# Product 6's weights multiplied by the gate on GpSimd, the last scaling on two engines, and one group of sums moved to GpSimd

## The chip, the cores and the metric

The kernel runs on one core of a Trainium2 chip. The metric is device time in microseconds; 957.09 is the median of three runs of the kernel before (956.73 to 957.37). The engines are TensorE (PE in the profile, its weight loads PEld), VectorE (DVE), ScalarE (ACT), GpSimd (POOL) and SyncE (SP), which here only issues DMA transfers.

## What is computed

One layer of a diffusion backbone on 512 tokens of 1024 channels with 256 context tokens. The attention and convolution ahead of the last part are left out here; the change touches only the MLP at the end, where `ga2` is one gate for each channel:

```
x = x + ga1 * (y_lat @ w_o)
x = x + ga2 * (square(relu(modulate(x, g_norm2, sh2, sc2) @ w_up)) @ w_down)
return rmsnorm(x, g_final)
```

## The kernel before

All products of this part are float32, each as three matmuls of rounded parts: an operand is split into a high part (rounded to fp32r by ScalarE) and a low part (what is left, by VectorE), and `mm3` issues high x high, high x low, low x high. So each weight tile, 128x1024, is loaded by SyncE into one of four raw buffers (`NRAW`), rounded by ScalarE, subtracted by VectorE, and read by TensorE from one of five pairs of buffers (`NW`): `weights`, lines 126 to 135.

The two MLP products are done as 2x2 block schemes with seven products in the place of eight, so that sums of blocks are multiplied. In the **up stage** (some 636 to 798 us) `left_sums` (line 1095) makes four sums of the normalized tokens' blocks for each of two pairs of token tiles, m = 0 and m = 1, by four VectorE subtractions or additions of 128x512, each depending on the one before for the first three; `keep` then splits them. The weights' own sums are made by `up_sum` (line 504): two on GpSimd (lines 510, 514), two on VectorE, in place.

The **down stage** (798 us to the end) has products n = 0 to 6, each of eight blocks of weights p = 0 to 7, here called p0 to p7, with 12 matmuls of 512 columns a block (`product`, line 1303). Sums of weights for n = 2, 3, 5 and 6 were made in device memory beforehand by `weight_sums`; `down_weights` (line 489) loads the right one. The stream of weights runs three blocks ahead in program order, and four raw buffers and five split buffers set how far ahead a load, a rounding and a subtraction can start. Left parts (`ap`) are split from the activations in `left_parts` in the same way, on the same two engines.

Product 6 adds only to tokens of the upper half (token tiles 2 and 3) and channels 0 to 511. Its last four blocks (`LAST`) are kept, and TensorE runs them first for token tile 2 (`ps_dd`), then for channels 0 to 255 of token tile 3, then, in a bank of their own (`ps_e`), for channels 256 to 511. Behind each, VectorE multiplies the sum in PSUM by the gate (`ada[5][0]`), adds it to the residual `x1`, ScalarE squares and sums for the norm, VectorE multiplies by `g_final`. `rstd_col` gives the reciprocal root as two factors, `y3` and `t3`, and two VectorE instructions scale the token tile's halves by both; SyncE issues the store of half 0 and ScalarE that of half 1 (lines 1379 to 1405).

Where nothing else is said, the order of the instructions on an engine is set when the program is built, from readiness and priorities, so it need not be the order of the lines. `tc.high_priority` moves instructions forward; `pinned` keeps some in the order of the lines.

Of the kernel before, what the change touches and what calls it, by code (L numbers as in the profile page):

```python
# [8 lines left out]
F32 = mybir.dt.float32  # L9
# [3 lines left out]
AF = mybir.ActivationFunctionType  # L13
ALU = mybir.AluOpType

P = 128
# [34 lines left out]
def hybrid_block_kernel(  # L51
# [6 lines left out]
    nc = tc.nc  # L58
    x, ctx, w_ada, w_in = x[0], ctx[0], w_ada[0], w_in[0]
    conv_w, w_conv_out, w_gla_out, w_o = conv_w[0], w_conv_out[0], w_gla_out[0], w_o[0]  # L60
    w_up, w_down, b_in, b_ada, out = w_up[0], w_down[0], b_in[0], b_ada[0], out[0]

    const = es.enter_context(tc.tile_pool(name="const", bufs=1))
    sp = es.enter_context(tc.tile_pool(name="sp", bufs=4))
# [25 lines left out]
    act, dve, pe = Engine(nc.scalar), Engine(nc.vector), Engine(nc.tensor)  # L90
# [4 lines left out]
    def kblk(name, dt=F32):  # L95
        return kp.tile([P, 512], dt, tag="kb", name=name)
# [6 lines left out]
    def psum(name):  # L103
        return pp.tile([P, 512], F32, tag="ps", name=name)

    def raw_tile(name):
        return wp.tile([P, 1024], F32, tag="raw", name=name, bufs=NRAW)
# [4 lines left out]
    def split(src, hi, lo, keep=False):  # L112

        for ins in (act.copy(out=hi, in_=src),
                    dve.tensor_tensor(out=lo, in0=src, in1=hi.bitcast(F32), op=ALU.subtract)):
            if keep:
                pinned(ins)
# [5 lines left out]

    latest = [None]

    def weights(name, src):

        raw = raw_tile("r_" + name)
        a, b = src.shape[1], src.shape[2]
        nc.sync.dma_start(out=raw.rearrange("p (a b) -> p a b", a=a), in_=src)  # L130
        hi = wp.tile([P, 1024], F32R, tag="hi", name="h_" + name)
        lo = wp.tile([P, 1024], F32R, tag="lo", name="l_" + name)
        split(raw, hi, lo, name == "up")
        latest[0] = lo
        return hi.rearrange("p (a b) -> p a b", a=a), lo.rearrange("p (a b) -> p a b", a=a)
# [29 lines left out]
    def rstd_col(name, first, last, n):  # L165

        b, v, y, t = (sp.tile([P, 1], F32, tag="rc_" + i, name=f"{i}_{name}") for i in "bvyt")
        dve.tensor_scalar(out=b, in0=first, scalar1=1.0 / n, scalar2=EPS, op0=ALU.mult, op1=ALU.add)
        act.activation(out=t, in_=last, func=AF.Ln, scale=1.0 / n, bias=b)
        act.activation(out=y, in_=t, func=AF.Exp, scale=-0.5)  # L170
        dve.scalar_tensor_tensor(out=v, in0=last, scalar=1.0 / n, in1=b, op0=ALU.mult, op1=ALU.add)
        dve.scalar_tensor_tensor(out=t, in0=y, scalar=y, in1=v, op0=ALU.mult, op1=ALU.mult)
        dve.tensor_scalar(out=t, in0=t, scalar1=-0.5, scalar2=1.5, op0=ALU.mult, op1=ALU.add)
        return y, t
# [75 lines left out]
    def sum_sq(dst, src, eng):  # L250
        junk = kp.tile([P, src.shape[1]], BF16, tag="junk", name="junk", bufs=2)
        if eng is act:
            act.activation(out=junk, in_=src, func=AF.Square, accum_out=dst)
        else:
            dve.scalar_tensor_tensor(out=junk, in0=src, scalar=1.0, in1=src, op0=ALU.mult, op1=ALU.mult, accum_out=dst)
# [131 lines left out]
    for s in range(2):  # L387
        dve.tensor_copy(out=lr_sel[:, 64 * s:64 * s + 48].rearrange("p (i r) -> p i r", i=3),
                        in_=sel[:, 16 * s:16 * s + 16].unsqueeze(1).to_broadcast([P, 3, RANK]))
    ps = psum("ps_c")  # L390
# [18 lines left out]
    ps = psum("ps_va")  # L409
# [17 lines left out]
    mod_w[1] = [ada_raw(1, q) for q in range(2)]  # L427
    normalized(x_tok, r_x, 0, P)
    wq = weights("q0", cols(w_in, C_Q))
    key_weights(1)  # L430
    Engine.ordered = False
# [37 lines left out]
    t_sum = [[dp.tile([P, 2, 512], F32, tag=f"t{i}_{p}", name=f"t{i}_{p}") for p in range(NFF // 4)] for i in range(4)]  # L469
# [3 lines left out]
    def quarter(j, hf, p):  # L473
        return rows(w_down, 16 * j + 2 * p, 512 * hf)

    def weight_sums():
# [7 lines left out]
        for i, p, src, add in todo:  # L484
            pinned(nc.gpsimd.tensor_copy(out=tick, in_=latest[0][0:1, 0:1].bitcast(F32)))
            pinned(nc.gpsimd.dma_start(out=t_sum[i][p], in_=src, **({"accum_op": ALU.add} if add else {})))  # L486
            yield

    def down_weights(n, p):

        if n in (2, 3, 5, 6):
            return weights("dn", t_sum[{2: 0, 3: 2, 5: 1, 6: 3}[n]][p])
        return weights("dn", quarter(*{0: (1, 0), 1: (0, 0), 4: (1, 1)}[n], p))

    up_raws = {}
# [69 lines left out]
    plan += [("up", cols(w_up, f * P)) for f in EARLY]  # L565
    hold = len(plan)
    plan += [("dn", lambda n=n, p=p: down_weights(n, p)) for n in range(7) for p in range(NFF // 4)]
    ws = Stream(plan, 3, hold)

# [240 lines left out]
    ada = {}  # L810
# [61 lines left out]
    def project(name, act=None):  # L872
        wt = ws.take(name)
        ps = tiles(name, act or h_lat, wt)
        ws.free()
        return ps
# [135 lines left out]
    for j in range(KT):  # L1012
        ps = project("go", og)
# [7 lines left out]
    x1 = [[None, None] for _ in range(MT)]  # L1021
# [73 lines left out]
    def left_sums(m):  # L1095

        (a11, a12), (a21, a22) = h2_f[m], h2_f[m + 2]
        s1, s2, s3, s4 = (kblk(f"s{i}").rearrange("p (k c) -> p k c", k=KH) for i in range(4))
        for out, a, b, op in ((s1, a21, a22, ALU.subtract), (s2, s1, a11, ALU.subtract),
                              (s4, s2, a12, ALU.add), (s3, a11, a21, ALU.subtract)):  # L1100
            dve.tensor_tensor(out=out, in0=a, in1=b, op=op)
        return s1, s2, s3, s4

    for m in range(MT):
# [14 lines left out]
    up_weights(0, "ua")  # L1119
    second_h(MT - 1, prev)  # L1120
    s_f = [left_sums(m) for m in range(2)]
    bp.release()
    mp = es.enter_context(tc.tile_pool(name="mp", bufs=1, reuse_waits="tile"))
# [173 lines left out]
    def block(ps, m, lp, wt, i, cs, start, stop, more=False):  # L1297
        mm3(ps, lp[0][:, i, m, :], lp[1][:, i, m, :], wt[0][:, i, cs], wt[1][:, i, cs], start, stop, more=more)
# [19 lines left out]
    def pair(name):  # L1318
        return [psum(name) for _ in range(2)]
# [55 lines left out]
    ps_d = pair("ps_dd")  # L1375
# [3 lines left out]
    for mi in range(2):  # L1379
        m, last = 2 + mi, mi == 1  # L1380
        pieces = [(0, 256), (256, 512)] if last else [(0, 512)]
        tmp = mp.tile([P, 2, 512], F32, tag="sp", name="tail", bufs=4)[:, 0, :] if last else kblk("tail")
        for i, (c0, c1) in enumerate(pieces):
            cs = slice(c0, c1)
            ps, x2, tt = ps_d[mi][:, cs], x1[m][0][:, cs], tmp[:, cs]
            if i == 1:

                dve.tensor_tensor(out=tt, in0=ps, in1=ada[5][0][:, cs], op=ALU.mult)
                dve.tensor_tensor(out=x2, in0=x2, in1=tt, op=ALU.add)
                ps = psum("ps_e")[:, cs]  # L1390
            for b in range(LAST):
                for j in range(2):
                    block(ps, mi, parts[b], wd[b], j, cs, i == 1 and b + j == 0, b == LAST - 1 and j == 1)
            with tc.high_priority(offset=100):
                dve.tensor_tensor(out=tt, in0=ps, in1=ada[5][0][:, cs], op=ALU.mult)
                dve.tensor_tensor(out=x2, in0=x2, in1=tt, op=ALU.add)
                sum_sq(ss3[:, m, i + 1:i + 2], x2, act)
                if i == 1:
                    dve.tensor_tensor(out=ss3[:, m, 0:1], in0=ss3[:, m, 0:1], in1=ss3[:, m, 1:2], op=ALU.add)
                dve.tensor_tensor(out=x2, in0=x2, in1=gf[0][:, cs], op=ALU.mult)  # L1400
        with tc.high_priority(offset=100):
            y3, t3 = rstd_col("n3", ss3[:, m, 0:1], ss3[:, m, i + 1:i + 2], D)
        for hf in range(2):
            dve.tensor_scalar(out=x1[m][hf], in0=x1[m][hf], scalar1=y3, scalar2=t3, op0=ALU.mult, op1=ALU.mult)
            (nc.sync, act)[hf].dma_start(out=out[m * P:(m + 1) * P, hf * 512:(hf + 1) * 512], in_=x1[m][hf])


# [27 lines left out]
```

## Time and profile before

| | us |
|---|---|
| median of three runs | 957.09 |
| lowest, highest | 956.73, 957.37 |
| the profiled execution | 959.36 |
| its span, first to last instruction | 957.6 |
| TensorE busy in it | 940.1 |
| VectorE busy | 710.2 |
| ScalarE busy | 536.2 |
| GpSimd busy | 164.8 |

The profile shows one execution; its own time is 1.8 us longer than its span and 2.3 us over the median. Times in the rows are microseconds from the span's start, engines have the names PE, PEld, DVE, ACT, POOL and SP. `r_dn`, `h_dn` and `l_dn` are a down weight tile as loaded, its high and its low part; `x1b` is the residual, `acc` the gate, `gf` the final norm's weights, `x_tmp` and `tail` products with the gate. A matmul's end is modelled, and pipelined matmuls overlap in the rows. What ended an engine's idle time stands in brackets behind a row.

### The profile page before, as it was taken

How to read it: one execution, taken by the hardware profiler on the slowest of the kernel's cores; microseconds unless marked ns; L12 is line 12 of the kernel's file. 1: busy time of each engine (PE TensorE's matmuls, PEld its weight loads, DVE VectorE, ACT ScalarE, POOL GpSimd, SP SyncE). 2: the span in 40 equal slices, each digit the busy share in tenths (PEclk: the TensorE clock that was granted, in tenths of full speed). 3: DMA queues.
4: the chain of work that ended last, by engine and by line, in shares of the span. 5: the costliest groups of instructions: out<-in, count | busy, mean ns of one | idle time of the engine just before them, and what ended most of it. 6: DMA issues, size and time to landing. Idle time of an engine off the chain costs nothing.

```text
span 957.6 us, 14834 instructions
## 1 busy us (share of the span) xinstructions
PE 940.1 (98%) x5555; PEld 800.1 (84%) x5555; DVE 710.2 (74%) x1170; ACT 536.2 (56%) x1008; POOL 164.8 (17%) x231
## 2 busy tenths in 40 slices
PE   6999999999999999999999999999999999999996
PEld 4678888788888888888888888899999998888886
DVE  5366685888598859977566484688768778899896
ACT  5476453745565556743543332478777687656662
POOL 8011022132112200002000000122445540000000
PEclk9999999999999999999999999999999999999999
DMA  9784072989648843636538466322557859655661
GB/s 288 225 293 169 5 250 74 233 188 192 172 132 215 172 120 103 206 98 181 184 95 261 130 216 202 130 88 63 189 169 177 188 128 309 227 191 190 196 220 44
DMA packets 162040, 165.51 MB, mean 173 GB/s; under 512 B 7524, under 2 KB 126416, under 8 KB 161712
## 3 DMA queue, kind: packets, MB, share of 16 engines
q1 hardware_dynamic: 147248, 124.94, 43.3%
q0 software_dynamic: 13568, 37.53, 15.9%
q10 hardware_dynamic: 1152, 2.10, 0.6%
q8 instruction: 43, 0.70, 0.3%
q14 instruction: 29, 0.24, 0.1%
HBM read 160.35 MB, written 37.75 MB: 207 GB/s over the span
## 4 chain that ended last, share of the span: by engine, by line
PE 91%; DVE 3%; DMA 3%; ACT 1%; issue 1%; SPq 0%; POOL 0%; DVEq 0%; POOLq 0%; ACTq 0%
PE ps_ua L83 8%; PE ps_da L83 7%; PE ps_v L83 6%; PE ps_c L83 5%; PE ps_ga L83 5%; PE ps_b L83 5%; PE ps_xa L83 5%; PE ps_r L83 5%; PE ps_y L83 5%; PE ps_db L83 5%; PE ps_gb L83 5%; PE ps_go L83 5%; PE ps_uc L83 4%; PE ps_co L83 4%; PE ps_dc L83 2%; PE ps_k L83 2%
## 5 line engine op out<-in xcount | busy, mean ns | idle before, releaser
L83 ACT CAST h_dn<-r_dn 128x1024 fp32r<-128x1024 f32 x56 | 59.0, 1054 | 48.0 <-PE ps_da L83 20.5
L83 DVE TENSOR_TENSOR l_dn<-r_dn,h_dn 128x1024 fp32r<-128x1024 f32 x56 | 68.1, 1221 | 14.7 <-ACT h_dn L83 14.4
L83 PE MATMUL ps_da<-h_dn,ap 128*128 128x512 f32 x192 | 59.6, 389 | 0.0
L83 DVE SCALAR_TENSOR_TENSOR acc<-wa,silu_c,acc 128x512 f32<-128x512 f32 x64 | 45.8, 747 | 12.4 <-DMA wa<-in_w_ada_dram 10.1
L83 PEld LDWEIGHTS ps_da<-h_dn,ap 128*128 128x128 f32 x192 | 36.0, 188 | 7.5
L486 POOL DMA_DIRECT2D t<-in_w_down_dram x48 | 40.3, 864 | 4.0 <-issue 3.9
L83 PE MATMUL ps_db<-h_dn,ap 128*128 128x512 f32 x128 | 39.8, 389 | 0.0
L83 PE MATMUL ps_da<-l_dn,ap 128*128 128x512 f32 x96 | 37.3, 389 | 0.0
L83 DVE TENSOR_TENSOR ap<-ug,ap 128x512 fp32r<-128x512 f32 x56 | 36.2, 685 | 0.0
L514 POOL TENSOR_TENSOR r_up<-r_up,r_up 128x512 f32<-128x512 f32 x14 | 24.3, 1737 | 48.3 <-DVE r_up L83 42.8
L83 ACT CAST ap<-ug 128x512 fp32r<-128x512 f32 x56 | 31.9, 617 | 0.3 <-DVE t_n L83 0.3
L1067 POOL DMA_DIRECT2D x<-x x8 | 4.4, 545 | 155.1 <-DVE x L83 152.3
L83 PEld LDWEIGHTS ps_db<-h_dn,ap 128*128 128x128 f32 x128 | 24.0, 188 | 4.9
L510 POOL TENSOR_TENSOR r_up<-r_up,r_up 128x512 f32<-128x512 f32 x14 | 25.9, 1852 | 6.2 <-DMA r_up<-in_w_up_dram 6.2
L83 PE MATMUL ps_v<-h_v,hh 128*128 128x512 f32 x64 | 25.8, 403 | 0.0
L83 PE MATMUL ps_xa<-hh,h_xa 128*128 128x512 f32 x64 | 25.5, 398 | 0.0
L83 PE MATMUL ps_ga<-hh,h_ga 128*128 128x512 f32 x64 | 25.4, 397 | 0.0
L83 PE MATMUL ps_b<-hh,h_b 128*128 128x512 f32 x64 | 25.4, 396 | 0.0
L83 PE MATMUL ps_c<-hh,h_c 128*128 128x512 f32 x64 | 25.3, 396 | 0.0
L83 PE MATMUL ps_co<-yah,h_co 128*128 128x512 f32 x64 | 25.2, 394 | 0.0
L83 PE MATMUL ps_r<-hh,h_r 128*128 128x512 f32 x64 | 25.1, 392 | 0.0
L83 PE MATMUL ps_y<-h_wo,yh 128*128 128x512 f32 x64 | 25.1, 392 | 0.0
(526 smaller groups left out, 3391.3 us busy)
## 6 DMA issues: line engine op xcount, KB each, us to landing
t<-in_w_down_dram POOLq DMA_DIRECT2D x48, 512.0 KB, 7.9
wa<-in_w_ada_dram SPq DMA_DIRECT2D x32, 512.0 KB, 4.1
r_up<-in_w_up_dram SPq DMA_DIRECT2D x32, 512.0 KB, 4.2
r_dn<-t SPq DMA_DIRECT2D x32, 512.0 KB, 4.1
r_dn<-in_w_down_dram SPq DMA_DIRECT2D x24, 512.0 KB, 4.4
wa<-in_w_ada_dram SPq DMA_DIRECT2D x32, 256.0 KB, 4.7
t<-t POOLq DMA_DIRECT2D x16, 512.0 KB, 5.6
r_v<-in_w_in_dram SPq DMA_DIRECT2D x8, 512.0 KB, 5.0
```

The lines of the kernel that those rows point to most:

```text
L83: ins = op(*args, **kwargs)
L486: pinned(nc.gpsimd.dma_start(out=t_sum[i][p], in_=src, **({"accum_op": ALU.add} if add else {})))
L510: pinned(nc.gpsimd.tensor_tensor(out=b0, in0=a0, in1=b0, op=ALU.add))
L514: pinned(nc.gpsimd.tensor_tensor(out=a0, in0=b1, in1=a0, op=ALU.subtract))
L1067: nc.gpsimd.dma_start(out=x1_d[m][:, hf, :], in_=x1[m][hf])
```

## The change

Three edits. (1) Product 6's weights are multiplied by the gate in their raw buffer, by two GpSimd instructions of 128x512 for each of the eight blocks, between the load and the rounding; the sums in PSUM of product 6 are then added to the residual without a product with the gate. (2) For the last token tile the two factors of the reciprocal root are multiplied with each other first, and then VectorE scales half 0 and ScalarE half 1. (3) `left_sums` runs on GpSimd for m = 0 and stays on VectorE for m = 1.

```diff
--- before.py
+++ after.py
@@ -123,11 +123,13 @@
 
     latest = [None]
 
-    def weights(name, src):
+    def weights(name, src, change=None):
 
         raw = raw_tile("r_" + name)
         a, b = src.shape[1], src.shape[2]
         nc.sync.dma_start(out=raw.rearrange("p (a b) -> p a b", a=a), in_=src)
+        if change:
+            change(raw)
         hi = wp.tile([P, 1024], F32R, tag="hi", name="h_" + name)
         lo = wp.tile([P, 1024], F32R, tag="lo", name="l_" + name)
         split(raw, hi, lo, name == "up")
@@ -486,10 +488,14 @@
             pinned(nc.gpsimd.dma_start(out=t_sum[i][p], in_=src, **({"accum_op": ALU.add} if add else {})))
             yield
 
+    def gated(raw):
+        for i in range(2):
+            nc.gpsimd.tensor_tensor(out=raw[:, i * 512:(i + 1) * 512], in0=raw[:, i * 512:(i + 1) * 512], in1=ada[5][0], op=ALU.mult)
+
     def down_weights(n, p):
 
         if n in (2, 3, 5, 6):
-            return weights("dn", t_sum[{2: 0, 3: 2, 5: 1, 6: 3}[n]][p])
+            return weights("dn", t_sum[{2: 0, 3: 2, 5: 1, 6: 3}[n]][p], gated if n == 6 else None)
         return weights("dn", quarter(*{0: (1, 0), 1: (0, 0), 4: (1, 1)}[n], p))
 
     up_raws = {}
@@ -1098,7 +1104,7 @@
         s1, s2, s3, s4 = (kblk(f"s{i}").rearrange("p (k c) -> p k c", k=KH) for i in range(4))
         for out, a, b, op in ((s1, a21, a22, ALU.subtract), (s2, s1, a11, ALU.subtract),
                               (s4, s2, a12, ALU.add), (s3, a11, a21, ALU.subtract)):
-            dve.tensor_tensor(out=out, in0=a, in1=b, op=op)
+            (nc.gpsimd if m == 0 else dve).tensor_tensor(out=out, in0=a, in1=b, op=op)
         return s1, s2, s3, s4
 
     for m in range(MT):
@@ -1379,29 +1385,33 @@
     for mi in range(2):
         m, last = 2 + mi, mi == 1
         pieces = [(0, 256), (256, 512)] if last else [(0, 512)]
-        tmp = mp.tile([P, 2, 512], F32, tag="sp", name="tail", bufs=4)[:, 0, :] if last else kblk("tail")
         for i, (c0, c1) in enumerate(pieces):
             cs = slice(c0, c1)
-            ps, x2, tt = ps_d[mi][:, cs], x1[m][0][:, cs], tmp[:, cs]
+            ps, x2 = ps_d[mi][:, cs], x1[m][0][:, cs]
             if i == 1:
 
-                dve.tensor_tensor(out=tt, in0=ps, in1=ada[5][0][:, cs], op=ALU.mult)
-                dve.tensor_tensor(out=x2, in0=x2, in1=tt, op=ALU.add)
+                dve.tensor_tensor(out=x2, in0=x2, in1=ps, op=ALU.add)
                 ps = psum("ps_e")[:, cs]
             for b in range(LAST):
                 for j in range(2):
                     block(ps, mi, parts[b], wd[b], j, cs, i == 1 and b + j == 0, b == LAST - 1 and j == 1)
             with tc.high_priority(offset=100):
-                dve.tensor_tensor(out=tt, in0=ps, in1=ada[5][0][:, cs], op=ALU.mult)
-                dve.tensor_tensor(out=x2, in0=x2, in1=tt, op=ALU.add)
+                dve.tensor_tensor(out=x2, in0=x2, in1=ps, op=ALU.add)
                 sum_sq(ss3[:, m, i + 1:i + 2], x2, act)
                 if i == 1:
                     dve.tensor_tensor(out=ss3[:, m, 0:1], in0=ss3[:, m, 0:1], in1=ss3[:, m, 1:2], op=ALU.add)
                 dve.tensor_tensor(out=x2, in0=x2, in1=gf[0][:, cs], op=ALU.mult)
         with tc.high_priority(offset=100):
             y3, t3 = rstd_col("n3", ss3[:, m, 0:1], ss3[:, m, i + 1:i + 2], D)
+        if last:
+            dve.tensor_tensor(out=t3, in0=t3, in1=y3, op=ALU.mult)
         for hf in range(2):
-            dve.tensor_scalar(out=x1[m][hf], in0=x1[m][hf], scalar1=y3, scalar2=t3, op0=ALU.mult, op1=ALU.mult)
+            if last and hf:
+                act.activation(out=x1[m][hf], in_=x1[m][hf], func=AF.Copy, scale=t3)
+            elif last:
+                dve.tensor_scalar(out=x1[m][hf], in0=x1[m][hf], scalar1=t3, scalar2=None, op0=ALU.mult)
+            else:
+                dve.tensor_scalar(out=x1[m][hf], in0=x1[m][hf], scalar1=y3, scalar2=t3, op0=ALU.mult, op1=ALU.mult)
             (nc.sync, act)[hf].dma_start(out=out[m * P:(m + 1) * P, hf * 512:(hf + 1) * 512], in_=x1[m][hf])
 
 

```

## Rows read from the trace of the kernel before

**Rows 1.** The page, first part: busy us, share of the span and instructions of each engine.

```profile
PE 940.1 (98%) x5555; PEld 800.1 (84%) x5555; DVE 710.2 (74%) x1170; ACT 536.2 (56%) x1008; POOL 164.8 (17%) x231
```

**Rows 2.** Chain that ended last, in order of time: start us, us, engine, tile, matmuls.

```profile
906.55 21.76 PE ps_da L83 x96
```

**Rows 3.** Timeline of PE in the up stage: start us, us, instruction [idle before <-releaser].

```profile
661.17 0.39 PE L83 MATMUL ps_uc<-s4h,h_ub 128*128 128x256 f32 x1 [0.72 <-ACT uq L83]
```

**Rows 4.** Timeline of SP, product 6's first load; last line of the view of tile r_dn.

```profile
909.75 0.32 SPq L130 DMA_DIRECT2D r_dn<-t  x1
...
DMA to landing us min/median/max: 3.1/4.3/7.5
```

**Rows 5.** Timeline of ACT: rounding of block p7's weights.

```profile
936.55 1.05 ACT L83 CAST h_dn<-r_dn 128x1024 fp32r<-128x1024 f32 x1 [1.46 <-issue]
```

**Rows 6.** Timeline of DVE: low parts of the weights p4 and p5, and of p7.

```profile
935.17 2.35 DVE L83 TENSOR_TENSOR l_dn<-r_dn,h_dn 128x1024 fp32r<-128x1024 f32 x2
...
939.78 1.22 DVE L83 TENSOR_TENSOR l_dn<-r_dn,h_dn 128x1024 fp32r<-128x1024 f32 x1
```

**Rows 7.** Timeline of PE: start of block p7, and the last matmul of the kernel.

```profile
942.88 0.62 PE L83 MATMUL ps_dd<-h_dn,ap 128*128 128x512 f32 x2
...
950.10 0.28 PE L83 MATMUL ps_e<-h_dn,ap 128*128 128x256 f32 x1
```

**Rows 8.** Busy us by stretch: PE, PEld, DVE, ACT, POOL, PEclk; last: tile ps_da alone.

```profile
636.00:661.00 25.00, 24.44 (x205) 24.24 (x203) 23.14 (x34) 19.39 (x42) 8.96 (x3) 1.00 0.25 71
912.85:941.00 28.15, 28.15 (x126) 23.32 (x125) 26.51 (x38) 15.27 (x22) 0.00 (x0) 1.00 0.51 169
28.00:32.00 4.00, 2.72 (x29) 1.42 (x27) 1.73 (x5) 1.94 (x4) 0.00 (x0) 1.00 1.11 337
32.00:36.00 4.00, 4.00 (x13) 3.17 (x12) 2.06 (x4) 3.16 (x6) 0.00 (x0) 0.57 1.02 316
...
912.85:941.00 28.15, 15.46 (x69) 12.47 (x67) 2.64 (x4) 1.00 0.51 169
```

**Rows 9.** Timeline of POOL: four of its 28 additions and subtractions in the up stage.

```profile
637.75 4.97 POOL L510 TENSOR_TENSOR r_up<-r_up,r_up 128x512 f32<-128x512 f32 x1 [5.54 <-DMA r_up<-in_w_up_dram]
...
656.25 2.28 POOL L510 TENSOR_TENSOR r_up<-r_up,r_up 128x512 f32<-128x512 f32 x1
...
670.95 1.31 POOL L510 TENSOR_TENSOR r_up<-r_up,r_up 128x512 f32<-128x512 f32 x1
...
769.10 2.27 POOL L510 TENSOR_TENSOR r_up<-r_up,r_up 128x512 f32<-128x512 f32 x1
```

**Rows 10.** Timeline of DVE around three of them.

```profile
640.88 0.68 DVE L83 TENSOR_TENSOR s<-s,h2f 128x512 f32<-128x512 f32 x1
...
642.08 1.19 DVE L83 TENSOR_TENSOR h2l<-h2f,h2h 128x512 fp32r<-128x512 f32 x1 [0.51 <-ACT h2h L83]
...
657.41 2.21 DVE L83 TENSOR_TENSOR l_uc<-r_up,h_uc 128x1024 fp32r<-128x1024 f32 x1
...
770.15 0.41 DVE L83 TENSOR_TENSOR uq<-uq,ps_ub 128x256 f32<-128x256 f32 x1
```

**Rows 11.** Groups of DVE, 912.94 to 941.00: line, operation, tiles xcount | busy us, mean ns.

```profile
L83 DVE TENSOR_TENSOR x1b<-x1b,x_tmp 128x512 f32<-128x512 f32 x4 | 2.6, 680 | 0.0
...
L83 DVE TENSOR_TENSOR x_tmp<-q,acc 128x512 f32<-128x512 f32 x2 | 1.4, 682 | 0.0
...
L83 DVE TENSOR_TENSOR x1b<-x1b,gf 128x512 f32<-128x512 f32 x2 | 1.3, 684 | 0.0
```

**Rows 12.** Timeline of DVE behind the last matmul; one ACT instruction of 128x512.

```profile
950.71 0.42 DVE L83 TENSOR_TENSOR tail<-ps_e,acc 128x256 f32<-128x256 f32 x1
...
952.73 0.22 DVE L83 SCALAR_TENSOR_TENSOR t_n<-y_n,v_n 128x1 f32<-128x1 f32 x1
...
953.17 1.00 DVE L83 TENSOR_SCALAR x1b<-x1b,y_n,t_n 128x512 f32<-128x512 f32 x2
...
946.18 0.63 ACT L83 ACTIVATE junk<-x1b 128x512 bf16<-128x512 f32 x1 [8.58 <-DVE x1b L83]
```


## The prediction, written before the change was run

> **What bounds the kernel now.** I read the page's first part, then the chain that ended last, then single stretches. TensorE is busy for 98% of the span [rows 1], and in the down stage the chain holds nothing but its matmuls, as in the 21.76 us of product 5 from 906.55 on [rows 2]. So a change there costs time when it makes TensorE wait, and saves time only behind the last matmul. The up stage has one TensorE wait left, 0.72 us at 661.17 [rows 3].
>
> The edit that matters is the multiplication of product 6's weights. Their way is: load, round to the high part on ScalarE, subtract to the low part on VectorE, matmul. Block p0's load is issued at 909.75 and such loads land after 3.1 us at the earliest [rows 4], so at 912.85. The last block's (p7) rounding starts at 936.55 and takes 1.05 [rows 5], its low part starts at 939.78 and ends at 941.00 [rows 6], and TensorE begins p7 at 942.88 [rows 7]. p7's low part is first read by the second matmul, 0.23 later: a slack of 2.1 us. Between 912.85 and 941.00, 28.15 us, TensorE never stops and VectorE is busy for 26.51 [rows 8].
>
> **What a GpSimd instruction costs VectorE.** GpSimd does the same form today, a 128x512 add of two tiles of the on-chip memory. Undisturbed it takes 1.31 us [rows 9]. At 656.25 one takes 2.28 [rows 9], and VectorE's low-part subtraction at 657.41, which has two such inputs as well, takes 2.21 [rows 10] instead of the 1.22 of this shape [rows 6]: VectorE loses 0.99 us to it. At 637.75 a GpSimd add that starts in a run of VectorE subtractions takes 4.97 us [rows 9]; the run's last starts at 640.88, the add comes through in VectorE's idle 0.51 us behind it, and the next subtraction, at 642.08, takes 1.19 where its form takes 0.68 [rows 10]. At 770.15 a VectorE instruction with one input from PSUM keeps its 0.41 us while a GpSimd add, from 769.10 to 771.37, lies over it [rows 9, 10]. So the two engines take turns where both read two tiles of the on-chip memory, at about 1.0 us of VectorE's time for a GpSimd instruction, and GpSimd has to wait while VectorE runs without a gap.
>
> **The change, part by part.**
>
> *Weights times gate.* 8 blocks by 2 halves are 16 GpSimd instructions, 16 x 0.99 = 15.8 us of shared reading. VectorE's own is 26.51 less the 2.64 that read PSUM [rows 8], 23.9. Together 39.7 us have to pass in a stretch of 28.15, an overrun of 11.55. Less the slack of 2.1 this is 9.45. Behind the last GpSimd product p7 must still be rounded (1.05 [rows 5]), when neither side has other work for the shared reading: 10.5. Below that: 0, if the 16 x 1.31 = 21.0 us ran freely in the 23.7 us between 912.85 and p7's rounding. Above: 16 x 1.31 taken from VectorE in full, 21.0 + 23.9 - 28.15 - 2.1 + 1.05 = 15.7. I take 10.5, since row and count are of this very form. Queued behind a GpSimd product on GpSimd is only the next one; on ScalarE everything behind the block's rounding waits (the next left parts and squared sums), and VectorE's low part behind that; the low part frees the buffer of the load four blocks on, so p4 to p7 land later as well. No load is added, and SP's queue keeps its order. TensorE is hurt from p4 on: five pairs of buffers let the first blocks be split up to four blocks, 10.9 us, ahead.
>
> The row at 637.75 and a page of the Trainium skill part here. SBUF — State Buffer, section "SBUF: two separate sides", says that the pair of ports is a lock and that whoever starts first gets it for a whole instruction; the subtraction of 640.88 started 3.1 us later than the add of 637.75 and yet went first. By the page's order GpSimd would never wait for more than one VectorE instruction, its products would finish sooner, and the roundings behind the last would lie beside VectorE work: the term would be 9.45 and not 10.5.
>
> *Clock.* If TensorE stands still its clock may fall. At 28 to 32 us TensorE was busy for 2.72 of 4 us, and the granted clock of the next 4 us reads 0.57 [rows 8], nearly all at the lower level, 1.2 GHz: (1 - 0.57) x 4 = 1.7 us lost. Here p3 would end near 939, 3 x 1.36 before p7's start of 942.88 (1.36 being half of a block's 2.72, since in the tail token tile 2 goes first), and p4 begin some 8 us later. Part of the loss would hide, as p5 to p7 wait for their low parts anyway. Between 0 and 1.7 I take 0.8.
>
> *Left sums.* Four VectorE subtractions of 0.68 (the form of [rows 11]) leave, 2.7 us; four GpSimd ones come, 4 x 0.99 = 4.0: the shared reading grows by 1.3 us in a stretch where VectorE is busy for 23.14 of 25.00 us [rows 8]. Behind them in GpSimd's queue stands the add of 637.75, behind the sums the splits, and VectorE's and ScalarE's chain to the wait at 661.17. If the shorter VectorE queue wins, the 0.72 us goes; if all GpSimd time lands on the chain, +4.0. I take +0.8: the net growth of 1.3, less a part for the stretch's 1.86 us of idle VectorE, some of which it can use.
>
> *Tail.* The last matmul ends at 950.38 [rows 7]. VectorE begins the product with the gate at 950.71, as its earlier two products of this kind keep it busy, and the add that follows 0.46 later [rows 12]. Both earlier products and this one go, so the add can begin at 950.41: -0.76. One more 128x1 instruction comes, at 0.25 (the pitch from the one at 952.73 to the next), and the two scalings, 1.00 in sequence on VectorE from 953.17 [rows 12], become one on VectorE beside one on ScalarE of 0.63 (the same shape at 946.18 [rows 12]): -0.37. Together -0.9. The two stores behind them are issued on the same queues as now. What the third product that goes (token tile 2's) saves counts for nothing: TensorE's matmuls of token tile 3 cover it.
>
> **Sum.** 10.5 + 0.8 + 0.8 - 0.9 = +11.2 us. The profiled execution took 959.36 us for a span of 957.6, so it would be 970.6; it stands 2.3 us over the median of the runs, 957.09, and from that I come to **968.3 us**. Own range of this case: low 957.09 + 8 - 0.7 + 0 - 0.9 = 963.5 (a GpSimd instruction at 0.83 us: 13.3 + 23.9 - 28.15 - 2.1 + 1.05 = 8.0); high, with half of the way to the upper ends, 957.09 + 13.1 + 1.3 + 2.4 - 0.9 = 973.0.
>
> **Rivals.**
>
> *It fits (not slower).* The 21.0 us of GpSimd work lie in 23.7 us, and both engines run side by side: then only the tail is left, 956.2, and 955.5 if the wait at 661.17 goes as well. It decides if a GpSimd product costs VectorE less than 0.33 us: then 16 x 0.33 + 23.9 is no more than 28.15 + 2.1 - 1.05. For it: undisturbed, each block needs 2.62 us, and TensorE takes 2.72 for one (21.76 / 8 [rows 2]). Against: the 2.21 and the 4.97, and VectorE's only 1.64 us of idle.
>
> *VectorE's order softens it.* The finishing of product 5 (four adds, two products and two scalings with both inputs on chip, 2.6 + 1.4 + 1.3 = 5.3 us [rows 11]) now stands ahead of p4's low part at 935.17 [rows 6]. If it came behind the splits in the changed program, 5.3 of the overrun would fall where TensorE doesn't wait: 10.5 - 5.3 + 0.8 - 0.9 = +5.1, 962.2. For it: nothing but product 6's end needs these. Against: their inputs are ready at 927.9, sooner than any late weight, so an order by readiness puts them first.
>
> *Left sums alone decide.* If the weights fit but the left sums do not, +4.0 - 0.9 = +3.1, 960.2; one step of the above, at a small chance.
>
> **How the numbers follow.** Forecast 0.63, order 0.13, left sums alone 0.04, it fits 0.20. No change that a measurement tells is within 0.2%, 1.9 us. It fits gives 956.2, within that; faster needs more than the tail and the 0.72 together (1.6), so 0.04 of its 0.20, and same 0.16. Slower 0.80. The range 956 to 974 takes in the rivals down to 956.2 and the forecast's own range; it leaves out the fastest 0.04 and some 0.12 of the forecast beyond 974, where two upper ends would meet.
>
> **What would show it.** Right: TensorE idle by some 9 us in the last product, before p4 to p7, waiting for l_dn; VectorE's l_dn of p0 to p7 well over 1.22 us each; GpSimd products with a median near 2 us; VectorE full from 912 to 952. Wrong: GpSimd products of 1.31 beside l_dn of 1.22. In the tail the last add right behind the last matmul, and both stores issued within 0.1 us. For the left sums the wait that stood at 661.17, longer or gone.

## The result, and the profile after

The changed kernel takes **973.36 us** (median; 973.0 to 976.85) beside 956.91 for the kernel before: ratio 1.0178, 95% interval 1.0157 to 1.0199. On a second chip it took 971.57 beside 957.83, ratio 1.0137 (1.0113 to 1.0161). Forecast were 968.3 and slower: the sign is right, the mechanism in the main, and the loss of 11.2 was sized too small; measured are 16.5 and 13.7. The first of the two times lies 0.4 above the forecast's own range (963.5 to 973.0), the second within it. The two profiled executions of the changed kernel, with spans of 971.2 and 968.6, are called the first and the second trace.

How the traces are compared matters here. Taking the start of each matmul in one trace less its start in the trace of before, the first 40 us alone differ between executions by 0.7 to 2.9 us, in kernels that do the same there (the profiled execution of before has the slow stretch of [rows 8] at 32 us, the others don't). From 40 us on the offset changes only at a few places, and it is counted from there below (us):

| | left sums (at 668) | down products 0 to 5 | last product, to its last matmul | behind it |
|---|---|---|---|---|
| changed, first trace | +1.8 | +0.7 | +13.6 | -0.55 |
| changed, second trace | +1.9 | 0.0 | +12.5 | -0.55 |

The first trace's sum is 15.5, the second's 13.8. The last product holds most of both. The 0.7 is a step at 796.46, where TensorE waits 0.35 us for an `ap` of ScalarE; it isn't the left sums', since a kernel further down that has them on VectorE shows such a wait too (0.34 at 794.33), and why it comes only in some executions is open. The page of after, part 1 and the new group of part 5 (busy us, mean ns | idle before, releaser); they answer to [rows 1]:

```profile
PE 942.1 (97%) x5555; PEld 800.1 (82%) x5555; DVE 720.4 (74%) x1162; ACT 537.2 (55%) x1009; POOL 201.0 (21%) x251
...
L493 POOL TENSOR_TENSOR r_dn<-r_dn,acc 128x512 f32<-128x512 f32 x16 | 31.8, 2021 | 127.2 <-DMA r_dn<-t 124.7
```

VectorE has 8 instructions fewer and is busy for 10.2 us more. In the last product TensorE waits for it; first the timeline of PE of before, where p4's low part is first read, then that of after, waits only (start, us [idle before <- releaser]):

```profile
939.26 0.39 PE L83 MATMUL ps_dd<-l_dn,ap 128*128 128x512 f32 x1
```

```profile
938.26 0.50 PE L83 MATMUL ps_dd<-l_dn,ap 128*128 128x512 f32 x1 [0.96 <-DVE l_dn L83]
...
950.85 0.79 PE L83 MATMUL ps_dd<-l_dn,ap 128*128 128x512 f32 x1 [9.57 <-DVE l_dn L83]
```

The first wait is for the low part of block p3, the second for that of p4. In the second trace the two waits are 0.31 and 9.56. What VectorE did until then, timeline of DVE of after:

```profile
923.05 1.28 DVE L83 TENSOR_TENSOR ap<-ug,ap 128x512 fp32r<-128x512 f32 x2
927.85 1.23 DVE L83 TENSOR_TENSOR l_dn<-r_dn,h_dn 128x1024 fp32r<-128x1024 f32 x1 [3.51 <-ACT h_dn L83]
931.35 1.23 DVE L83 TENSOR_TENSOR l_dn<-r_dn,h_dn 128x1024 fp32r<-128x1024 f32 x1 [2.27 <-ACT h_dn L83]
932.49 3.48 DVE L83 TENSOR_TENSOR ap<-ug,ap 128x512 fp32r<-128x512 f32 x2
935.89 2.31 DVE L83 TENSOR_TENSOR l_dn<-r_dn,h_dn 128x1024 fp32r<-128x1024 f32 x1
...
940.53 2.85 DVE L83 TENSOR_TENSOR x1b<-x1b,x_tmp 128x512 f32<-128x512 f32 x2
943.30 1.75 DVE L83 TENSOR_TENSOR x_tmp<-q,acc 128x512 f32<-128x512 f32 x1
944.97 0.68 DVE L83 TENSOR_TENSOR x_tmp<-ps_da,acc 128x512 f32<-128x512 f32 x1
...
949.58 2.34 DVE L83 TENSOR_TENSOR l_dn<-r_dn,h_dn 128x1024 fp32r<-128x1024 f32 x2
```

The pair `ap` at 932.49 takes 3.48 where the pair at 923.05, undisturbed, takes 1.28, the single `l_dn` at 935.89 2.31 and not 1.22, `x_tmp` from `q` 1.75 and not 0.68: each instruction loses 1.07 to 1.10 us. The `x_tmp` at 944.97, which reads PSUM, keeps its 0.68, and the pair of `l_dn` at 949.58, behind the last GpSimd product, its 2.34 [rows 6]. GpSimd's products in the view of tile r_dn of after (ns min/median/max):

```profile
L493 POOL TENSOR_TENSOR r_dn<-r_dn,acc x16: 1290/1728/5796, 913.5 to 946.1; 128x512 f32<-128x512 f32 x16
```

The one of 5.8 us began at 919.69, while VectorE ran without a gap from 918.86 to 924.3. The roundings behind it came late, and for them VectorE stands idle 3.51 and 2.27 us in the rows above. The clock, after, by stretch (columns as in [rows 8], the granted clock is the third from the right):

```profile
944.00:948.00 4.00, 0.00 (x0) 0.00 (x0) 4.00 (x4) 1.25 (x3) 3.85 (x3) 0.73 0.00 0
948.00:952.00 4.00, 1.15 (x3) 0.96 (x4) 4.00 (x7) 1.36 (x2) 0.00 (x0) 0.50 0.00 0
952.00:956.00 4.00, 4.00 (x11) 3.13 (x10) 3.40 (x4) 0.00 (x0) 0.00 (x0) 0.50 0.00 0
956.00:960.00 4.00, 4.00 (x24) 3.44 (x24) 0.69 (x1) 0.36 (x1) 0.00 (x0) 0.99 0.00 0
```

TensorE stands still from 941.3; the granted clock falls to 0.50, the lower level of 1.2 GHz, and is still there for 5 us of matmuls: 11 in the stretch 952 to 956, against 24 in the next.

At the left sums, timeline of PE of after:

```profile
638.94 0.39 PE L83 MATMUL ps_u<-h2h,l_up 128*128 128x256 f32 x1 [0.23 <-DVE l_up L83]
642.87 0.39 PE L83 MATMUL ps_u<-h2l,h_up 128*128 128x256 f32 x1 [0.91 <-DVE h2l L83]
645.16 0.39 PE L83 MATMUL ps_u<-h2l,h_up 128*128 128x256 f32 x1 [0.60 <-DVE h2l L83]
```

The wait of [rows 3] is gone, and these three came. The tail, timelines of DVE, ACT and the two issuing queues of after; the last matmul starts at 964.29:

```profile
966.64 0.16 DVE L83 TENSOR_TENSOR t_n<-t_n,y_n 128x1 f32<-128x1 f32 x1
966.84 0.48 DVE L83 TENSOR_SCALAR x1b<-x1b,t_n 128x512 f32<-128x512 f32 x1
...
966.84 0.72 ACT L83 ACTIVATE x1b<-x1b,t_n 128x512 f32<-128x512 f32 x1 [0.71 <-DVE t_n L83]
967.59 0.34 ACTq L83 DMA_DIRECT2D out_dram<-x1b  x1
967.35 0.34 SPq L1415 DMA_DIRECT2D out_dram<-x1b  x1
```

### The profile page after: what moved, and what is told of

The parts are those of the page before. It is cut to its first block, busy times and chain, and to the rows that moved or that the text cites. A ratio compares the mean times of both kernels' runs of the same rounds, so it can differ in the third digit from the quotient of the medians.

```text
span 971.2 us, 14863 instructions
## 1 busy us (share of the span) xinstructions
PE 942.1 (97%) x5555; PEld 800.1 (82%) x5555; DVE 720.4 (74%) x1162; ACT 537.2 (55%) x1009; POOL 201.0 (21%) x251
## 4 chain that ended last, share of the span: by engine, by line
PE 86%; DVE 5%; DMA 3%; issue 3%; ACT 1%; POOL 1%; SPq 0%; DVEq 0%; POOLq 0%; ACTq 0%
PE ps_ua L83 8%; PE ps_v L83 6%; PE ps_c L83 5%; PE ps_ga L83 5%; PE ps_b L83 5%; PE ps_xa L83 5%; PE ps_r L83 4%; PE ps_y L83 4%; PE ps_gb L83 4%; PE ps_go L83 4%; PE ps_da L83 4%; PE ps_db L83 4%; PE ps_co L83 4%; PE ps_uc L83 4%; PE ps_dc L83 2%
## 5 line engine op out<-in xcount | busy, mean ns | idle before, releaser
L83 DVE TENSOR_TENSOR l_dn<-r_dn,h_dn 128x1024 fp32r<-128x1024 f32 x56 | 70.1, 1257 | 19.5 <-ACT h_dn L83 19.2
L493 POOL TENSOR_TENSOR r_dn<-r_dn,acc 128x512 f32<-128x512 f32 x16 | 31.8, 2021 | 127.2 <-DMA r_dn<-t 124.7
L83 DVE TENSOR_TENSOR ap<-ug,ap 128x512 fp32r<-128x512 f32 x56 | 38.3, 721 | 0.0
L520 POOL TENSOR_TENSOR r_up<-r_up,r_up 128x512 f32<-128x512 f32 x14 | 24.4, 1739 | 47.0 <-DVE r_up L83 30.9
L824 POOL MEMSET acc<- 128x512 f32 x8 | 4.0, 527 | 107.9 <-PE ps_o L83 73.4
```

Source lines behind the costliest of these rows:

```text
L83: ins = op(*args, **kwargs)
L493: nc.gpsimd.tensor_tensor(out=raw[:, i * 512:(i + 1) * 512], in0=raw[:, i * 512:(i + 1) * 512], in1=ada[5][0], op=ALU.mult)
L520: pinned(nc.gpsimd.tensor_tensor(out=a0, in0=b1, in1=a0, op=ALU.subtract))
L824: nc.gpsimd.memset(acc[hf], 0.0)
```

## The experiments

The theory of turns: a GpSimd instruction that reads the on-chip memory stops VectorE's instructions with two such inputs, VectorE is full in the last product, and so the loss appears as late low parts. Rivals: GpSimd's own time in the chain from load to low part; the order of VectorE's work; the other two edits. Each run below gives its median in us beside that of the kernel before on the same chip, and in brackets the 95% interval of the ratio.

**One edit at a time.** First the scaling alone (before + second edit):

```diff
+        if last:
+            dve.tensor_tensor(out=t3, in0=t3, in1=y3, op=ALU.mult)
         for hf in range(2):
...
+            if last and hf:
+                act.activation(out=x1[m][hf], in_=x1[m][hf], func=AF.Copy, scale=t3)
```

> The kernel before with the second edit alone (the last tile's scaling as one VectorE half and one ScalarE half). In the changed kernel the whole tail from the last matmul's end to the end of the span is 6.62 us against 7.22; the first edit takes two multiplications out of it, so the second can have at most a part of those 0.60. Theory (small gain, since the factor t3*y3 has to be made first on VectorE): 0.1 to 0.4 us faster, 956.5 to 956.8 against 956.9. Rival (ScalarE's half is slower than the VectorE instruction it replaces, with the extra product in front): 0.1 to 0.4 us slower.

957.9 beside 957.77, ratio 0.9997 (0.9985 to 1.0009): no difference that can be told by the time. The trace leans to the rival's side: from the last matmul's start to the end of the span 7.64 us against 7.49. Timeline of this kernel, last matmul at 949.34:

```profile
952.60 0.72 ACT L83 ACTIVATE x1b<-x1b,t_n 128x512 f32<-128x512 f32 x1 [0.67 <-DVE t_n L83]
953.35 0.34 ACTq L83 DMA_DIRECT2D out_dram<-x1b  x1
...
953.11 0.34 SPq L1412 DMA_DIRECT2D out_dram<-x1b  x1
```

Counted from the last matmul ScalarE's store goes out 0.10 us earlier than before (4.01 against 4.11) and SP's 0.13 later (3.77 against 3.64), and with the two closer together ScalarE's store lands 2.4 us after its issue and not 2.2.

Then the left sums alone (before + third edit):

```diff
-            dve.tensor_tensor(out=out, in0=a, in1=b, op=op)
+            (nc.gpsimd if m == 0 else dve).tensor_tensor(out=out, in0=a, in1=b, op=op)
```

> The kernel before with the third edit alone (left sums of two token tiles on GpSimd). Theory (what the matmuls' offsets show in the changed kernel: they fall behind by 2.1 to 2.3 at the left sums, get 0.5 back at the wait of 661, and lose 0.5 later): 1.8 to 2.5 us slower, 958.7 to 959.4 against 956.9. Rival (the prediction's own term, 0.8): 957.7. Rival (the offsets are two runs' differences and nothing else): 956.9.

959.85 beside 957.77, ratio 1.0018 (1.0007 to 1.0028), a loss of 1.7 (0.7 to 2.7): by the time alone the rival's 0.8 is not excluded. The trace is +1.7 from 668 on and stays there to the last matmul. Its waits of TensorE from 600 on (waited for: us in total, times, longest):

```profile
PE ps_u L83 <- DVE l_up L83: 1.3, 1, 1.3
PE ps_u L83 <- DVE h2l L83: 0.9, 1, 0.9
```

With smaller delays TensorE falls 2.7 us behind there, and 0.9 come back where the wait of [rows 3] was. The first edit was run by itself too (the changed kernel with the other two undone):

> The first edit alone (weights multiplied on GpSimd; left sums on VectorE; scaling as before). Theory (the edits add up, and the first holds nearly all): 973.4 less 2.2 for the left sums, plus 0.3 for the scaling: 971.5, between 970.5 and 972.5. Rival (the left sums' backlog, carried to the end, makes part of the first edit's price): under 969.

969.47 beside 957.77, ratio 1.0122 (1.0102 to 1.0142), 1.0 under the range given. Its trace has +12.7 in the last product, as the second trace (12.5), with waits of 9.9 in total:

```profile
PE ps_dd L83 <- DVE l_dn L83: 9.9, 2, 9.5
```

So the edits do add up (12.7 and 1.7), and the first trace was the dearer one. Behind the last matmul this kernel takes 6.77 us, 0.71 less than before.

**Half of the products.**

```diff
-        for i in range(2):
+        for i in range(1):
             nc.gpsimd.tensor_tensor(out=raw[:, i * 512:(i + 1) * 512], ...
```

> The changed kernel with 8 products on GpSimd in place of 16 (only the first 512 of a block's 1024 columns are multiplied; the other half of the last down product is left without its gate). Theory of turns (each product costs a VectorE instruction with two operands in SBUF 1.06 us, and VectorE's sum sets the last weights' arrival): 8 x 1.06 = 8.5 less of VectorE's time, which takes the wait of 9.57 to about 1 and that of 0.96 to none, and most of the slow clock's 2.55 with them: 973.4 - 8.5 - 0.96 - 2.3 = 961.7, between 960 and 964. Rival (GpSimd's first product behind a load sets it, as a latency of each block): one product less in a chain of eight blocks' loads, 1.3 to 2.3 less: 971 to 972.

962.14, ratio 1.0045 (1.0027 to 1.0062), inside the theory's 960 to 964. The last product loses 4.4 us where the changed kernel loses 12.5 to 13.6; one wait is left, and slower matmuls behind it (granted clock 0.66 from 942 to 946) make the rest:

```profile
PE ps_dd L83 <- DVE l_dn L83: 2.5, 1, 2.5
```

**GpSimd time without reading.**

```diff
-        for i in range(2):
-            nc.gpsimd.tensor_tensor(out=raw[:, ...], in0=raw[:, ...], in1=ada[5][0], op=ALU.mult)
+        for i in (0, 1, 0, 1, 0):
+            nc.gpsimd.memset(raw[:, i * 512:(i + 1) * 512], 1.0)
```

> The changed kernel with each block's two products replaced by five GpSimd fills of 128x512 of the same raw tile (this leaves the last product's weights out: they become 1). GpSimd still stands between the load and the cast of each block, for about five times half a us, but it reads nothing. Theory of turns (the price is VectorE's, paid for what GpSimd reads while VectorE reads two operands of SBUF): VectorE's instructions keep their lengths, no wait of several us for the last weights, clock unbroken: 956.9 + 2.2 (left sums) - 0.7 (tail) = 958.4, between 957.5 and 960. Rival (GpSimd's step in the chain load, product, cast, remainder is what is late): about as the changed kernel, 968 to 973.

959.5 beside 958.41, ratio 1.0011 (0.9999 to 1.0023), as the theory said. The last product loses 0.0. The view of tiles r_dn on GpSimd and l_dn on VectorE (ns min/median/max):

```profile
L493 POOL MEMSET r_dn<- x40: 525/529/539, 913.7 to 935.4; 128x512 f32 x40
...
L83 DVE TENSOR_TENSOR l_dn<-r_dn,h_dn x11: 1216/1220/1226, 913.7 to 940.7; 128x1024 fp32r<-128x1024 f32 x11
```

GpSimd is busy for 5 x 0.53 = 2.6 us between load and rounding of each block, what two undisturbed products take, and nobody is late: the chain has the room for GpSimd's own time. It had none for the product of 5.8 us in the first trace, which waited for VectorE. Neither engine's instructions are stretched here.

**VectorE makes the products.** The edit: `nc.gpsimd.tensor_tensor` becomes `dve.tensor_tensor` in `gated`.

> The changed kernel with the 16 products of the weights done by VectorE itself. Theory of turns: VectorE gets 16 x 0.60 = 9.6 of work and loses the 16 x 1.06 = 17 of turns, 7.4 less, so of the waits of 9.57 + 0.96 some 3.1 stay, with up to 1.3 of slow clock: 956.9 + 2.2 - 0.7 + 3.1 + 0.6 = 962.1, between 960 and 965. Rival (VectorE's sum of work is the bound and GpSimd did take work off it): slower than the changed kernel, over 974.

964.41 beside 958.41, ratio 1.006 (1.0038 to 1.0082), within the range. Its 16 products take 0.69 each, and all else keeps its length:

```profile
L83 DVE TENSOR_TENSOR r_dn<-r_dn,acc x16: 683/685/687, 919.9 to 948.7; 128x512 f32<-128x512 f32 x16
```

TensorE waits 1.2 us in the last product. Its tail's matmuls stand in another order in this program, and behind the last of them come 8.7 us in place of before's 7.5, so only the waits are read. The 16 take 11 us of VectorE's time; given to GpSimd, the same job cost it more (the sums are below).

**Order.** The finishing of product 5 moved, in the text, behind `wd = [ws.take("dn") ...]`.

> The changed kernel with the finishing of the fifth down product written behind the taking of the last four blocks, so that VectorE's queue has it between the last remainders of weights, not all of it ahead of them. Theory of turns (VectorE's work ahead of the very last remainder stays nearly the same, and only the first of the four comes sooner): 1 to 6 us less than 973.4, 967 to 972. Rival (order: the 11.4 us of finishing ahead of the fifth block's remainder is the price): nearly all of the 9.57 gone, and the clock's 2.55 with it, 961 to 963.

970.34, ratio 1.0125 (1.0106 to 1.0143): the theory's range; the rival of order falls. p4's low part now comes early, and the wait moves on to later blocks, timeline of PE:

```profile
937.46 0.50 PE L83 MATMUL ps_dd<-l_dn,ap 128*128 128x512 f32 x1 [0.89 <-DVE l_dn L83]
941.48 0.50 PE L83 MATMUL ps_dd<-l_dn,ap 128*128 128x512 f32 x1 [1.01 <-DVE l_dn L83]
948.72 0.80 PE L83 MATMUL ps_dd<-l_dn,ap 128*128 128x512 f32 x1 [5.57 <-DVE l_dn L83]
```

The last product loses 11.2 us, 1.3 to 2.4 less than in the changed kernel.

**The clock.**

```diff
     wd = [ws.take("dn") for _ in range(LAST)]
+    for _ in range(38):
+        pe.matmul(ps_c[0], ones_r, ones_r.unsqueeze(1).to_broadcast([P, 4, P]), start=True, stop=True)
```

> The changed kernel with 38 matmuls of 128x512 on constants put on TensorE between the third and the fourth last blocks of the last product, some 8.1 us of the wait of 9.57; nothing reads what they make. Theory (TensorE's idleness there lets the clock fall, and the slow stretch costs 2.55): the granted clock stays at 1.00, and the time falls by 2.55 less what the remainders of the last two blocks are late at full speed, about 0.7: 1.9 less, 971.5, between 970.8 and 972. Rival (the clock's price is hidden, since the last weights' remainders come at 953.7 and 955.4 whatever the clock): 973.2 to 973.5.

970.34 beside 958.41, ratio 1.0120 (1.0102 to 1.0138); its interval overlaps the changed kernel's second one, so the trace has to decide. PE in the wait, and the clock in the stretches that answer to those of after:

```profile
941.31 8.79 PE L83 MATMUL ps_dc<-ones_r 128*128 128x512 f32 x38
...
951.30 0.50 PE L83 MATMUL ps_dd<-l_dn,ap 128*128 128x512 f32 x1 [0.97 <-DVE l_dn L83]
```

```profile
946.00:950.00 4.00, 4.00 (x20) 3.23 (x18) 4.00 (x5) 2.61 (x4) 2.35 (x2) 1.00 0.00 0
950.00:954.00 4.00, 3.02 (x14) 2.17 (x12) 4.00 (x6) 0.00 (x0) 0.00 (x0) 1.00 0.00 0
```

The clock stays at 1.00. p4's low part is first read 10.4 us late here, in the second trace 10.3; from there to the last matmul this kernel loses 0.7 more, the second trace 2.2 and the first 2.6. So 2.2 to 2.6 are lost with the slow clock, and 1.5 to 1.9 of it would be saved at full speed, where TensorE overtakes the low parts of p6 and p7 again. The time itself lies 0.5 under the range given.

**Size of one GpSimd instruction.** One product of 128x1024 for a block in place of two of 128x512.

> The changed kernel with one GpSimd product of 128x1024 for each block in place of two of 128x512 (8 instructions, the same arithmetic). Theory of work (VectorE stands still for as long as GpSimd's product itself takes, so the loss goes with the elements): VectorE loses the same 17 in all, and the wait of 9.57 before the fifth block stays within 1.5: 971.5 to 974.5. Rival (a toll for each change of turn, whatever the size): 8 x 1.06 = 8.5 less of VectorE's time, and the time of the kernel with half of the products, 961 to 964.

972.86 beside 957.83, ratio 1.0154 (1.0127 to 1.0181): the loss goes with the elements. TensorE's waits sum to 10.4 as before (10.5), but the one before p4 is 5.35, outside what was expected, with another of 5.02 before p3. Timeline of DVE:

```profile
926.79 5.67 DVE L83 TENSOR_TENSOR l_dn<-r_dn,h_dn 128x1024 fp32r<-128x1024 f32 x2 [3.37 <-ACT h_dn L83]
932.39 5.66 DVE L83 TENSOR_TENSOR ap<-ug,ap 128x512 fp32r<-128x512 f32 x2
937.97 3.36 DVE L83 TENSOR_TENSOR l_dn<-r_dn,h_dn 128x1024 fp32r<-128x1024 f32 x1
```

The `ap` pair loses 4.4 us to two products, 2.2 each, twice the 1.07 to 1.10 of a product of half the size.

**One input on GpSimd.**

```diff
-            nc.gpsimd.tensor_tensor(out=..., in0=raw[...], in1=ada[5][0], op=ALU.mult)
+            nc.gpsimd.tensor_scalar(out=..., in0=raw[...], scalar1=1.5, scalar2=None, op0=ALU.mult)
```

> The changed kernel with the 16 products replaced by 16 GpSimd multiplications of the same 128x512 tiles by a constant (one operand in SBUF in place of two; the gate of the last down product is left out, its weights are times 1.5). Theory A (any GpSimd instruction that reads SBUF takes turns with VectorE, as the 1x1 copies on GpSimd do that last 0.17 alone and 1.11 beside VectorE): as the changed kernel or a few us less, if the instruction by itself is shorter than a product: 964 to 974. Theory B (only two operands on GpSimd make VectorE wait): no wait for the last weights, as with the fills: 957.5 to 960.5.

962.33 beside 957.83, ratio 1.0042 (1.0029 to 1.0056): both expectations missed, the truth lies between. The last product loses 2.7. The view of tile r_dn, and one `l_dn` of the timeline of DVE:

```profile
L493 POOL TENSOR_SCALAR r_dn<-r_dn x16: 1489/1647/2447, 913.3 to 940.6; 128x512 f32<-128x512 f32 x16
...
918.25 1.62 DVE L83 TENSOR_TENSOR l_dn<-r_dn,h_dn 128x1024 fp32r<-128x1024 f32 x1
```

A GpSimd instruction with one input takes 1.65, as long as a product, but costs VectorE 0.40 and not 1.07. So the loss isn't the length of GpSimd's instruction; it goes with what it reads. Why one input costs 0.40 and not half of 1.07 is open.

**The products elsewhere.** The kernel before, with the weights multiplied ahead of time:

```diff
+            if n in (1, 4) and b % 2 == 1:
+                gate_early((n == 4) * 4 + b // 2)
...
+    def gate_early(p):
+        r = mp.tile([P, 2, 512], F32, tag="sp", name="gt", bufs=4)
+        nc.gpsimd.dma_start(out=r, in_=t_sum[3][p])
+        gated(r.rearrange("p a b -> p (a b)"))
+        nc.gpsimd.dma_start(out=t_sum[3][p], in_=r)
```

> The kernel before with the first edit's result by another way: each of the eight blocks of the last down product's weights is fetched from its place in device memory by GpSimd's own queue during the second and the fifth down products, multiplied by the gate on GpSimd there, and written back, so that nothing stands between load and cast in the last product; scaling and left sums as before. Theory of turns (the price is paid only where VectorE has no idle time: it is busy 125 of the 140 us from 790 to 930, and TensorE waits for nothing there, since weights are made blocks ahead): between nothing and 2 us lost in the down products, and the tail 0.78 shorter, as in the kernel with the first edit alone: 956.1 to 958, likeliest 956.2. Rival (16 turns of 1.06 are 17 us against 15 of idle time, so the loss comes out at TensorE wherever they stand): 959 to 964.

964.31 beside 957.83, ratio 1.0068 (1.0044 to 1.0091): the rival's side, 0.3 above its range. The last product loses nothing, but 7.8 us are lost before 860. TensorE's longest wait there, the stretches 810 to 850, and the second of them in the kernel before (columns as in [rows 8]; the last two are the busy share of the DMA engines and GB/s):

```profile
845.92 0.54 PE L83 MATMUL ps_dc<-l_dn,ap 128*128 128x512 f32 x1 [3.24 <-DVE l_dn L83]
```

```profile
810.00:830.00 20.00, 20.00 (x90) 16.57 (x89) 14.74 (x12) 12.78 (x17) 13.92 (x14) 1.00 0.95 341
830.00:850.00 20.00, 16.76 (x67) 13.39 (x67) 19.93 (x14) 9.43 (x13) 12.33 (x10) 0.91 0.82 294
```

```profile
830.00:850.00 20.00, 20.00 (x90) 16.56 (x89) 19.97 (x24) 12.65 (x18) 0.00 (x0) 1.00 0.52 173
```

The products were not spread as the edit reads: 14 of the 16 ran between 806 and 847, six of these from 835.6 on, where VectorE has no idle time before (19.97 of 20 us). So the run doesn't show what products cost beside an idle VectorE.

VectorE's idle 5 us at 810 to 830 are not used up, which the rival's account would ask. The DMA share is 0.95 and 0.82 (before: 0.78 and 0.52), and the weights' loads issued from 800 to 850 land after a median of 7.0 us where before it is 4.3. So the added transfers may have a part beside the turns; no run parts the two.

**The changed kernel again**, beside the last three:

> The changed kernel itself, on the same chip as the three beside it. Expected as on record, 973.4, between 972.5 and 975; in its trace the offset of its matmuls against the kernel before, counted from 40 us on (the first 40 us differ from run to run), is +1.8 at 668 and +16 at the last matmul; the offset of 0.6 more near 798 comes or doesn't, since two of five kernels with the same left sums showed it.

971.57, ratio 1.0137, 0.9 under the range given; by the trace +1.9, then +14.4 at the last matmul and not 16. The step near 798 doesn't come, and the wait before p3 is 0.31 in place of 0.96. None of these kernels beats the one before.

## Why the prediction was right, and where not

*Weights times gate, +10.5.* Right in size and in the main mechanism. p4's low part is first read 11.0 us late in the first trace (950.85 against 939.26, less the 0.6 that the whole trace was late by ahead of the last product) and 10.3 in the second, as in the kernel with this edit alone (10.3). A product costs VectorE 1.07 to 1.10 (predicted 0.99), for the reason given: half the products take the loss from 12.5 or more to 4.4, fills cost nothing. The bounds also did their work: the lower end, products running freely, is what the fills show, and products do not run freely. One row was misread: that of 942.88 [rows 7] merges two matmuls, the first of them p6's last, so p7 begins at 943.11, the slack is 2.3 and not 2.1, and the term would be 10.3.

Not all of the loss is VectorE's turns, though. Against their lengths in the kernel before, VectorE's instructions from 908 to 953 us lose 14.9 us in the second trace, in 15 of them, and VectorE is full. In the first they lose 9.7, in 10 of them, and VectorE stands idle for 5.8 us more, for roundings behind the product of 5.8 us; there it is GpSimd that waits for its turn, and the chain from load to low part is late. VectorE in the second trace, columns as in [rows 8]:

```profile
912.00:952.00 40.00, 30.12 (x125) 24.24 (x124) 40.00 (x38) 14.80 (x22) 29.92 (x16) 0.89 0.35 119
```

The prediction names this path (behind a block's rounding everything waits) but has no term for it. That both sums come to some 15 us is not explained, so for the first trace the term's size may be luck.

The two accounts that were weighed against each other, 9.45 and 10.5, lie about as far apart as the two traces do, so the time can't tell them apart. Their sign shows in the order, though. The Trainium skill, SBUF — State Buffer, section "SBUF: two separate sides", has the first starter take the pair of ports; mostly the trace agrees, with one VectorE instruction after each product, but the product of 5.8 us began at 919.69 and was passed by five VectorE instructions that began behind it. The second trace has no product over 2.34 us, so such starving comes and goes; why isn't known. The same section says that an instruction of VectorE with two such inputs is stopped only by a GpSimd instruction that reads: the fills agree, with `l_dn` at 1.22. Its hold of a whole instruction does not fit the run with one input, where VectorE loses 0.40 to instructions of 1.65.

*Order (rival, 962.2).* It fell. The order in the changed program was the forecast's, and the other order gives back 1.3 to 2.4 and not 5.3, because the work that is moved behind p4's low part then stands ahead of p7's.

*Clock, +0.8 of 0 to 1.7.* Sized too small: 2.2 to 2.6 are lost from p4 on, 1.5 to 1.9 more than in the kernel whose clock stays up. The step that failed took one stretch of 4 us at 0.57 as the most that can be lost. Here TensorE stood still for 9.6 us, and the matmuls ran at the lower level for 5 us behind that. The other half of the step, that late low parts hide a part, is right (0.7).

*Left sums, +0.8 of -0.7 to 4.0.* 1.7 to 1.9, inside the bounds. The steps that failed are the rebate of 0.5 for VectorE's 1.86 us of idle time and the price, 1.1 for a turn and not 0.99. Five instructions of VectorE lose 1.1 us each, four beside the left sums and the last beside the add that stands behind them in GpSimd's queue; timeline of DVE of after:

```profile
634.26 2.39 DVE L83 TENSOR_TENSOR h2l<-h2f,h2h 128x512 fp32r<-128x512 f32 x2
636.58 2.31 DVE L83 TENSOR_TENSOR l_up<-r_up,h_up 128x1024 fp32r<-128x1024 f32 x1
638.81 2.31 DVE L83 TENSOR_TENSOR l_ua<-r_up,h_ua 128x1024 fp32r<-128x1024 f32 x1
641.04 1.77 DVE L83 TENSOR_TENSOR h2l<-h2f,h2h 128x512 fp32r<-128x512 f32 x1
642.74 1.76 DVE L83 TENSOR_TENSOR s<-h2f 128x512 f32<-128x512 f32 x1
```

That is 5.5 for the 2.7 that left and the 0.5 that the add cost before [rows 10]: 2.3 net. TensorE falls 2.5 to 2.8 behind there and gets 0.7 to 0.9 back where the wait of [rows 3] was.

*Tail, -0.9.* -0.55. The products with the gate are worth 0.71 (forecast 0.76). The scaling, forecast at -0.12, is +0.15 in its own trace: ScalarE's half takes 0.72 (0.63 was taken from another instruction), SP's store waits for the added 128x1 product, and the second store lands later when both are issued 0.24 us apart.

*Level.* The two traces lie 1.7 us apart by their sums: of the 13.7 and 16.5 us the steps give 13.8 and 15.5, the step at 796 with its 0.7 among the latter; the rest of the first is within its executions' spread of 3.9.

*Signs named.* TensorE's idle 9 us before p4, product medians near 2 us (1.73), the last add right behind the last matmul (964.60 behind 964.29) and the end of the wait at 661 came. `l_dn` of p0 to p7 well over 1.22 did not: in the first trace only p3's is stretched (2.31), in the second p2's and p3's, and the others keep 1.21 to 1.23; the time was lost mostly in other instructions, `ap`, `x1b` and `x_tmp` among them. VectorE was full from 912 to 952 in the second trace only; the stores were 0.24 and not 0.1 apart.

## What to carry to other kernels

Ask of an idle engine not only whether it is idle, but what its instructions take from the busy one: here 16 products of GpSimd cost VectorE 15 us (in the first trace 5.8 of them as waiting), more than the 11 it takes to do them itself, to save 0.7 us behind the last matmul. Find the price in the trace first, as the length of the same VectorE form beside and away from a GpSimd instruction, and set it against the idle time of VectorE in that very stretch. When a wait of many us is forecast, put the clock's price behind it as well.

## What the runs showed that was not expected

A GpSimd fill of 128x512 (0.53 us) costs VectorE nothing, one with one input 0.40 us, one with two 1.07 to 1.10, while the last two last about as long (1.65 and 1.73 in the median). The size of VectorE's own instruction doesn't matter: one of 128x1 that began at 913.53, beside the first product, took 1.36 us and not 0.21. A store issued 0.24 us behind another lands 2.4 us after its issue; 0.47 us behind it, 2.2. The first 40 us of executions of like kernels differ by over 2 us, which is more than two of the three edits are worth: without an offset counted from a later matmul, single profiles would have misled.
